# A two-layer RWKV-7 / gated-attention trunk: other accumulators for half units, another order at the attention's entry, and the last scaling split over two engines

## The chip, the cores and the metric

The kernel runs on one core of one Trainium2 chip. The metric is the device time of one execution in microseconds (us). Three runs of the kernel before took 2380.53, 2381.64 and 2383.12 us; their median, 2381.64 us, is what the change is compared with.

## The reference

Sixteen learned tokens stand ahead of 256 real ones, so T = 272 columns go through two layers of width 2048, all in float32:

```
layer 0: h = h + rwkv7(rms_norm(h));  h = h + (relu(rms_norm(h) @ w1) ** 2) @ w2
layer 1: h = h + gla(rms_norm(h));    h = h + (relu(rms_norm(h) @ w1) ** 2) @ w2
out = rms_norm(h)[16:]

gla(x): q, k, v, gate, za = split(x @ w_in)          # za has 16 columns
        glog = log_sigmoid(za @ w_a2 + b_a) / 16      # forget gate of each key dimension
        chunks of 64 tokens: q*exp(cumsum glog), k*exp(-cumsum glog), causal products with v and the state
        out = (per-head norm(o) * silu(gate)) @ w_o
```

The hidden size of the feed-forward part is 8192. Layer 0 ends with the output projection of the RWKV mixer (`w_o`, 2048 x 2048); layer 1 begins with the projection `w_in`, whose last 16 columns (za) feed the forget gate.

## The kernel before

Activations lie transposed: 128 model dimensions on the partitions, tokens along the columns, 16 tiles of 128 dimensions. A product in float32 accuracy is made of three passes over split operands: each 128x1024 piece of weights comes from memory as `raw`, ScalarE rounds it to `hi` (L140), VectorE forms the rest `lo = raw - hi` (L141), and TensorE makes hi*x_hi, hi*x_lo and lo*x_hi (L163, L164, L165; L196 and L197 where two passes are joined). One such piece serves 24 matmuls, some 2.8 us. There are three `raw` buffers, refilled by SP's queue, whose transfers start in the order of that queue when the buffer is free, that is, when VectorE has made the `lo` of its last piece. `hi` and `lo` have two buffers, four inside the gated attention, where two pools take turns.

The order on each engine is fixed when the kernel is built: a scheduler takes the instructions by priority as its own model finds them ready, except inside blocks of manual order (TensorE through the whole RWKV part). `tc.high_priority(offset=...)` pulls the instructions inside it ahead in that choice. On the chip each engine works off its list in order; an instruction that waits holds all that follow it on its engine.

PSUM has eight accumulator banks: `pj` (two), `pm`, `pry` (one each), `pt` and `pu` (two each). A group of products writes one bank, and the next group on this bank waits until VectorE has read it.

**End of the RWKV mixer.** The output projection is cut into units. A half unit `outB(f)` (L907) adds up the last 8 of 16 input tiles for output tile f, on a `pj` bank. A unit `outQ(3, p)` takes 4 input tiles for the two output tiles 2p and 2p+1, on both `pj` banks. The tail of the list is `outB(0), outQ(3,4), outB(1), outB(2), outQ(3,5), outB(3)` and so on to `outB(7)`. Behind each group VectorE adds the bank to the residual (L300), and `done(f)` prepares the next layer's operand for tile f: ScalarE's x_hi (L239) and square (L250), VectorE's x_lo (L240) and the running sum `acc` of squares (L251).

**Entry of the gated attention.** `done` of the first feed-forward part prepares the attention's operand in the same way, and TensorE sums `acc` over the partitions (L255), from which ScalarE makes `rstd`. In `gla` (L1086) the weights `w_a2` of the forget gate are loaded first into a `raw` buffer and split into `wa2`, then za is projected (`pair(48)`), scaled by `rstd` (`zf`), split into `za`, and `gate(0)` and `gate(1)` multiply za by `wa2` on TensorE (L1117) and make the decay factors. Only then come the query and key projections of the first head, `proj(pair(0))` and `proj(pair(8))`.

**The end.** After the last feed-forward part the squares are summed on TensorE (L1316), ScalarE makes `rstd` (L231, L232), and VectorE multiplies the 16 tiles by it in six pieces (L1321); SP sends each piece out when it is made (L1322). GpSimd has no work there.

Of the kernel before, what the change touches and what calls it, by code (L numbers as in the profile page):

```python
# [10 lines left out]
F32 = mybir.dt.float32  # L11
F32R = mybir.dt.float32r
AF = mybir.ActivationFunctionType
ALU = mybir.AluOpType
# [4 lines left out]
P = 128  # L19
D = 2048  # L20
KT = D // P
NMETA = 16
SEQ = 256
T = NMETA + SEQ
# [30 lines left out]
class Kern:  # L55
# [242 lines left out]
    def rwkv(self, done):  # L298
        nc, tc, ap = self.nc, self.tc, self.ap
        tt = lambda o, a, b, op=ALU.mult: nc.vector.tensor_tensor(out=o, in0=a, in1=b, op=op)  # L300
        hres = self.hres
# [58 lines left out]
        pair = lambda w, f: [w[f, 0], w[f, 1]]  # L360
# [5 lines left out]
        with tc.manual_schedule(engines={ENG.PE, ENG.DVE, ENG.Activation}):  # L366
# [51 lines left out]
            for kt in range(KT):  # L418
                w = weight(kt)
                raw, hi, lo = w  # L420
# [484 lines left out]


        def outB(f):  # L907
            ps = self.pj()[:, :T]
            yield from units(yo[8:], 1, ps)
            tt(self.two(hres[:, f]), self.back(ps), self.two(loc[f]), ALU.add)  # L910
            done(f)
            yield
# [173 lines left out]
    def gla(self, x, rstd, hres, done):  # L1086
# [8 lines left out]
        nc.sync.dma_start(gc, ap["gcst"])  # L1095
        mG = gc[:, 0:T]
        mk = [gc[:80, 272:528], gc[:, 528:720], gc[:, 720:784]]
        raw = self.t(self.wp, [P, 1024], "raw", self.raw_bufs)
        nc.sync.dma_start(raw, ap["gla_w_a2"])
        wa2 = self.t(gp, [P, 1024], "wa2", 1, F32R)  # L1100
        nc.scalar.copy(wa2, raw)
        low = slice(64, 96)
        tt(wa2[low], raw[low], wa2[low].bitcast(F32), ALU.subtract)
        zf = self.t(gp, [P, T], "mn", 2)
        tt(self.two(zf), self.proj(pair(48), x, T), self.two(rstd))
        za = self.t(gp, [P, T], "za", 1, F32R)
        nc.scalar.copy(za, zf)
        low = slice(32, 64)
        tt(za[low], zf[low], za[low].bitcast(F32), ALU.subtract)
        rs = rstd[:, NMETA:]  # L1110
        oT = [self.t(self.x2p, [P, 2, T], "x", KT, F32R) for _ in range(KT)]
        c0, c1, c2, c3 = (NMETA + C * i for i in range(4))
# [23 lines left out]
            nc.scalar.activation(dec, dec, AF.Exp, scale=1.0 / TAU)  # L1136
            gates[j] = eb, enb, dec

        for j in range(2):
            gate(j)  # L1140
        for hd in range(GH):
            Q = self.t(gp, [P, 2, 7 * C], "Q", 2)
            KX = self.t(gp, [P, 2, 160 + 6 * C], "KX", 1)
            for dt in range(2):
                j = 2 * hd + dt
                eb, enb, dec = gates.pop(j)
                pq = self.proj(pair(j), x, SEQ, NMETA)
                q, last = Q[:, dt], [eb[:, o + C - 1 : o + C] for o in (c0, c1, c2)]
                qf = self.t(gp, [P, SEQ], "qf", 2)
                nc.vector.scalar_tensor_tensor(out=self.two(qf), in0=pq, scalar=HK ** -0.5, in1=self.two(rs), op0=ALU.mult,  # L1150
                                               op1=ALU.mult)
                tt(q[:, : 3 * C], qf[:, : 3 * C], eb[:, c0:c3])
                tt(q[:, 6 * C :], qf[:, 3 * C :], eb[:, c3:])
                nc.vector.tensor_copy(q[:, 3 * C : 4 * C], q[:, C : 2 * C])
                nc.vector.tensor_scalar(out=q[:, 4 * C : 5 * C], in0=q[:, 2 * C : 3 * C], scalar1=last[1], scalar2=None,
                                        op0=ALU.mult)
                nc.vector.tensor_scalar(out=q[:, 5 * C : 6 * C], in0=q[:, 6 * C :], scalar1=last[2], scalar2=last[1],
                                        op0=ALU.mult, op1=ALU.mult)
                pk = self.proj(pair(8 + j), x, T)
                ks = self.t(gp, [P, T], "ks", 2)  # L1160
                tt(self.two(ks), pk, self.two(rstd))
                kx = KX[:, dt]
                two = lambda x: x.rearrange("p (a t) -> p a t", a=2)
                run = kx[:, 160:]
                tt(kx[:, :NMETA], ks[:, :NMETA], dec[:, :NMETA])
                tt(kx[:, NMETA:80], ks[:, NMETA:c1], enb[:, NMETA:c1])
                tt(two(run[:, : 4 * C])[:, :, :C], two(ks[:, c1:c3]), two(enb[:, c1:c3]))
                tt(run[:, 5 * C :], ks[:, c3:], enb[:, c3:])
                tt(kx[:, 80:160], ks[:, :c1], dec[:, :c1])
                nc.vector.tensor_scalar(out=kx[:, 80 : 80 + NMETA], in0=kx[:, 80 : 80 + NMETA], scalar1=last[0], scalar2=None,  # L1170
                                        op0=ALU.mult)
                tt(run[:, C : 2 * C], ks[:, c1:c2], dec[:, c1:c2])
                nc.vector.tensor_scalar(out=run[:, 3 * C : 4 * C], in0=run[:, C : 2 * C], scalar1=last[2], scalar2=None,
                                        op0=ALU.mult)
                tt(run[:, 4 * C : 5 * C], ks[:, c2:c3], dec[:, c2:c3])
# [97 lines left out]
@with_exitstack  # L1273
def trunk(ctx, tc, ap):
    K = Kern(ctx, tc, ap)
    nc = tc.nc
    out, hres = ap["out"], K.hres
    st = {}

    def operand(gname, off, pool):  # L1280
        def f(kt):
            if kt == 0:
                p = pool()
                st["x"] = [K.t(p, [P, 2, T], "x", KT, F32R) for _ in range(KT)]
                st["acc"] = K.t(K.sp, [P, T], "acc")
            K.prep(K.sp, kt, hres[:, kt, off:], gname, st["x"][kt], st["acc"], T - off)
        return f

    def x2():
        K.x2p = K.sp = ctx.enter_context(tc.tile_pool(name="x2", bufs=1, side="right", reuse_waits="tile"))  # L1290
        return K.x2p

    K.rwkv(operand("norm_mlp0", 0, x2))
    rstd = K.accstd(K.sp, st["acc"], T)
    K.mlp(0, st["x"], rstd, hres, 0, operand("norm_mix1", 0, lambda: K.xp))
    rstd = K.accstd(K.sp, st["acc"], T)
    K.gla(st["x"], rstd, hres, operand("norm_mlp1", NMETA, lambda: K.xp))
    rstd = K.accstd(K.sp, st["acc"], SEQ)

    def last(kt):  # L1300
        if kt == 0:
            st["acc"] = K.t(K.sp, [P, T], "acc")
        h = hres[:, kt, NMETA:]
        if kt < KT - 1:
            K.sqacc(K.sp, kt, h, st["acc"], SEQ)
        else:
            st["sq"] = K.t(K.sp, [P, T], "sq")[:, :SEQ]
            nc.scalar.activation(st["sq"], h, AF.Square)  # L1308
        nc.scalar.mul(h, h, K.vec("norm_f", kt))

    fp = ctx.enter_context(tc.tile_pool(name="fin", bufs=1, side="right"))
    fin = K.t(fp, [P, KT - 2, SEQ], "fin")
    K.mlp(1, st["x"], rstd, hres, NMETA, last)
    ss = K.pm()[:, :SEQ]
    for i, x in enumerate((st["acc"][:, :SEQ], st["sq"])):
        nc.tensor.matmul(ss, K.ones, x, start=i == 0, stop=i == 1)  # L1316
    rstd = K.rstd_from(K.sp, ss, SEQ, 1.0 / D, NORM_EPS, "acc")
    for a, b in ((0, 1), (1, 3), (3, 6), (6, 10), (10, 14), (14, 16)):
        h = hres[:, a:b, NMETA:]
        y = fin[:, a:b] if b < KT else h  # L1320
        nc.vector.tensor_tensor(out=y, in0=h, in1=rstd.unsqueeze(1).to_broadcast([P, b - a, SEQ]), op=ALU.mult)  # L1321
        nc.sync.dma_start(out[:, a:b], y)  # L1322


# [89 lines left out]
```

## Time and profile before

| what | value |
|---|---|
| median of the three runs | 2381.64 us |
| profiled execution, its own time | 2381.23 us |
| its span, first to last instruction | 2379.0 us |
| TensorE busy in the span | 2346.9 us, 99% |
| VectorE busy | 1607.7 us, 68% |
| ScalarE busy | 1260.6 us, 53% |
| GpSimd busy | 12.1 us, 1% |
| granted TensorE clock | 0.999 |

The profiled execution took 2381.23 us, 2.2 us more than its span; what lies outside the span is start and end of the program. "Busy" of TensorE counts matmuls that overlap, so a small step between two matmuls' starts that is longer than usual is time lost, even where the row shows less idle. In the views below a row of the timeline gives the start, the duration, the engine, the line and the tiles (written <- read); brackets at its end give the idle time of the engine before it and who ended it. Rows of waits give: who waited for whom, the total in us, how often, the longest.

### The profile page before, as it was taken

What the parts mean: (1) busy time and instruction counts of PE and PEld (TensorE: products, weight loads), DVE (VectorE), ACT (ScalarE), POOL (GpSimd) and SP (SyncE); (2) the same over time, 40 slices, a digit from 0 to 9 for tenths busy, and PEclk for the clock granted to TensorE, in tenths of its full rate; (3) what the DMA queues carried; (4) which work ended last, traced back from release to release, by engine and by line L of the source; (5) the groups of instructions that cost most, each with busy time, mean ns of one, the idle gap of its engine ahead of it and who ended that gap; (6) DMA issues with size and microseconds to landing.
All of it is one profiled execution on the core that took longest, in us unless ns stands there. A gap on an engine that the chain in (4) does not pass through costs nothing. (4 is left out here: it accounts for less than half of the span.)

```text
span 2379.0 us, 48378 instructions
## 1 busy us (share of the span) xinstructions
PE 2346.9 (99%) x19849; PEld 2224.7 (94%) x19849; DVE 1607.7 (68%) x2702; ACT 1260.6 (53%) x2005; POOL 12.1 (1%) x37
## 2 busy tenths in 40 slices
PE   9999999999999999999999999999999999999998
PEld 8888888889999999999999999999999999999997
DVE  8868986848555555555556777767666666666666
ACT  6478645566555345345345556645555445445444
POOL 0000000000000000000000000000000000000000
PEclk9999999999999999999999999999999999999999
DMA  6469754435555555555555555445555656655554
GB/s 213 154 201 306 245 159 144 143 100 174 186 187 191 190 189 192 187 191 190 188 193 192 188 178 175 162 169 196 183 199 202 204 199 200 203 201 199 203 202 170
DMA packets 157005, 449.20 MB, mean 189 GB/s; under 512 B 33968, under 2 KB 49968, under 8 KB 156784
## 3 DMA queue, kind: packets, MB, share of 16 engines
q1 hardware_dynamic: 156784, 446.11, 56.5%
q8 instruction: 156, 2.56, 0.4%
q14 instruction: 65, 0.53, 0.1%
HBM read 429.93 MB, written 14.42 MB: 187 GB/s over the span
## 5 line engine op out<-in xcount | busy, mean ns | idle before, releaser
L141 DVE TENSOR_TENSOR lo<-raw,hi 128x1024 fp32r<-128x1024 f32 (+1 forms) x818 | 927.7, 1141 | 532.2 <-ACT hi L140 522.1
L140 ACT CAST hi<-raw 128x1024 fp32r<-128x1024 f32 (+1 forms) x818 | 794.1, 978 | 922.4 <-PE pj L164 534.1
L163 PE MATMUL pj<-x,hi 128*128 128x272 f32 (+1 forms) x2624 | 746.5, 284 | 2.6 <-DVE hres L300 1.7
L165 PE MATMUL pj<-x,lo 128*128 128x272 f32 (+1 forms) x2624 | 732.5, 279 | 4.4 <-DVE lo L141 4.3
L164 PE MATMUL pj<-x,hi 128*128 128x272 f32 (+1 forms) x2624 | 731.7, 279 | 0.2 <-DVE x L240 0.2
L163 PEld LDWEIGHTS pj<-x,hi 128*128 128x128 f32 x2624 | 496.9, 189 | 15.8 <-issue 8.2
L165 PEld LDWEIGHTS pj<-x,lo 128*128 128x128 f32 x2624 | 497.0, 189 | 7.0 <-DVE lo L141 6.6
L164 PEld LDWEIGHTS pj<-x,hi 128*128 128x128 f32 x2624 | 497.1, 189 | 2.9 <-issue 1.4
L196 PE MATMUL pj<-x,hi 128*128 128x512 f32 x1280 | 419.8, 382 | 0.1
L197 PE MATMUL pj<-x,lo 128*128 128x256 f32 x1280 | 348.7, 273 | 0.0
L196 PE MATMUL pj<-h,hi 128*128 128x512 f32 x1008 | 330.3, 382 | 0.0
L163 PE MATMUL pj<-h,hi 128*128 128x272 f32 (+1 forms) x1040 | 290.1, 279 | 0.0
L164 PE MATMUL pj<-h,hi 128*128 128x272 f32 (+1 forms) x1040 | 290.1, 279 | 0.0
L165 PE MATMUL pj<-h,lo 128*128 128x272 f32 (+1 forms) x1040 | 290.1, 279 | 0.0
L197 PE MATMUL pj<-h,lo 128*128 128x256 f32 x1008 | 274.8, 273 | 0.0
L196 PEld LDWEIGHTS pj<-x,hi 128*128 128x128 f32 x1280 | 241.9, 189 | 34.1 <-DVE x L1088 0.4
L197 PEld LDWEIGHTS pj<-x,lo 128*128 128x128 f32 x1280 | 245.8, 192 | 0.1
L196 PEld LDWEIGHTS pj<-h,hi 128*128 128x128 f32 x1008 | 190.5, 189 | 26.5
L163 PEld LDWEIGHTS pj<-h,hi 128*128 128x128 f32 x1040 | 196.6, 189 | 0.0
L164 PEld LDWEIGHTS pj<-h,hi 128*128 128x128 f32 x1040 | 196.6, 189 | 0.0
L165 PEld LDWEIGHTS pj<-h,lo 128*128 128x128 f32 x1040 | 196.6, 189 | 0.0
L197 PEld LDWEIGHTS pj<-h,lo 128*128 128x128 f32 x1008 | 193.5, 192 | 0.0
(281 smaller groups left out, 2083.7 us busy)
## 6 DMA issues: line engine op xcount, KB each, us to landing
raw<-mlp_w_d SPq DMA_DIRECT2D x512, 512.0 KB, 3.4
raw<-gla_in_d SPq DMA_DIRECT2D x98, 512.0 KB, 3.3
raw<-w_rkv_d SPq DMA_DIRECT2D x80, 512.0 KB, 3.9
raw<-gla_o_d SPq DMA_DIRECT2D x32, 512.0 KB, 3.3
raw<-w_r_d SPq DMA_DIRECT2D x16, 512.0 KB, 3.3
raw<-rw_oQ_d SPq DMA_DIRECT2D x16, 512.0 KB, 3.4
raw<-lora_d SPq DMA_DIRECT2D x8, 512.0 KB, 3.5
raw<-rw_oA_d SPq DMA_DIRECT2D x8, 512.0 KB, 3.8
```

The costliest lines, as they stand in the source:

```text
L140: nc.scalar.copy(hi[:, h], raw[:, h])
L141: nc.vector.tensor_tensor(out=lo[:, h], in0=raw[:, h], in1=hi[:, h].bitcast(F32), op=ALU.subtract)
L163: nc.tensor.matmul(out, hi[:, ws], xh, start=first, stop=False)
L164: nc.tensor.matmul(out, hi[:, ws], xl, start=False, stop=False)
L165: nc.tensor.matmul(out, lo[:, ws], xh, start=False, stop=last)
L196: nc.tensor.matmul(wide, hi[:, ws], xt, start=kt == 0, stop=False)
L197: nc.tensor.matmul(one, lo[:, ws], xt[:, 0], start=False, stop=kt == nk - 1)
```

## The change

Three edits in one kernel.

1. In `outB(f)` the accumulator is `pry` for odd f and `pm` for even f, in place of a `pj` bank. `outQ` keeps the two `pj` banks.
2. In `gla` the projection of za is called ahead of the load and split of `w_a2`, which get a raised priority; the scaling and split of za get a higher one. The first query projection is called before the gates, `gate(0)` behind it, and `gate(1)` behind the first key projection. The preparation of tile 15 (`done(15)`, at all three borders between parts) gets a raised priority.
3. The last scaling gives its piece of tiles 14 and 15 to GpSimd. VectorE keeps the other five pieces, and SP's queue holds the transfer of GpSimd's piece second instead of last.

```diff
         def outB(f):
-            ps = self.pj()[:, :T]
+            ps = (self.pry if f % 2 else self.pm)()[:, :T]
             yield from units(yo[8:], 1, ps)
...
-        raw = self.t(self.wp, [P, 1024], "raw", self.raw_bufs)
-        nc.sync.dma_start(raw, ap["gla_w_a2"])
-        wa2 = self.t(gp, [P, 1024], "wa2", 1, F32R)
-        nc.scalar.copy(wa2, raw)
-        low = slice(64, 96)
-        tt(wa2[low], raw[low], wa2[low].bitcast(F32), ALU.subtract)
         zf = self.t(gp, [P, T], "mn", 2)
-        tt(self.two(zf), self.proj(pair(48), x, T), self.two(rstd))
+        pz = self.proj(pair(48), x, T)
+        with tc.high_priority(offset=2000):
+            raw = self.t(self.wp, [P, 1024], "raw", self.raw_bufs)
+            nc.sync.dma_start(raw, ap["gla_w_a2"])
+            wa2 = self.t(gp, [P, 1024], "wa2", 1, F32R)
+            nc.scalar.copy(wa2, raw)
+            low = slice(64, 96)
+            tt(wa2[low], raw[low], wa2[low].bitcast(F32), ALU.subtract)
         za = self.t(gp, [P, T], "za", 1, F32R)
-        nc.scalar.copy(za, zf)
         low = slice(32, 64)
-        tt(za[low], zf[low], za[low].bitcast(F32), ALU.subtract)
+        with tc.high_priority(offset=3000):
+            tt(self.two(zf), pz, self.two(rstd))
+            nc.scalar.copy(za, zf)
+            tt(za[low], zf[low], za[low].bitcast(F32), ALU.subtract)
+        pq = self.proj(pair(0), x, SEQ, NMETA)
...
-        for j in range(2):
-            gate(j)
+        gate(0)
...
-                pq = self.proj(pair(j), x, SEQ, NMETA)
+                if j:
+                    pq = self.proj(pair(j), x, SEQ, NMETA)
...
                 pk = self.proj(pair(8 + j), x, T)
+                if j == 0:
+                    gate(1)
...
-            K.prep(K.sp, kt, hres[:, kt, off:], gname, st["x"][kt], st["acc"], T - off)
+            with tc.high_priority(offset=3000) if kt == KT - 1 else ExitStack():
+                K.prep(K.sp, kt, hres[:, kt, off:], gname, st["x"][kt], st["acc"], T - off)
...
-    for a, b in ((0, 1), (1, 3), (3, 6), (6, 10), (10, 14), (14, 16)):
+    for a, b in ((0, 1), (14, 16), (1, 3), (3, 6), (6, 10), (10, 14)):
         h = hres[:, a:b, NMETA:]
         y = fin[:, a:b] if b < KT else h
-        nc.vector.tensor_tensor(out=y, in0=h, in1=rstd.unsqueeze(1).to_broadcast([P, b - a, SEQ]), op=ALU.mult)
+        (nc.gpsimd if b == KT else nc.vector).tensor_tensor(out=y, in0=h, in1=rstd.unsqueeze(1).to_broadcast([P, b - a, SEQ]),
+                                                           op=ALU.mult)
         nc.sync.dma_start(out[:, a:b], y)
```

What the scheduler makes of it is seen in the lists of the engines. On VectorE at the entry of the attention, before (16723 and 16753 are the two halves of za's weights, `wa` is the split of `w_a2`, `hres` and x_15690 belong to tile 15, `acc` is the sum that TensorE's L255 waits for):

```order
L141 TENSOR_TENSOR lo_16724<-raw_16721,hi_16723 128x1024
L213 TENSOR_TENSOR hres_72<-pj_16633,hres_72 128x272
L141 TENSOR_TENSOR lo_16754<-raw_16751,hi_16753 128x1024
L1088 TENSOR_TENSOR wa_2342_16716<-raw_16714,wa_2342_16716 32x1024
L240 SCALAR_TENSOR_TENSOR x_15690<-hres_72,vecs_126,x_15690 128x272
L251 TENSOR_TENSOR acc_15691<-acc_15691,sq_16697 128x272
```

and now (16718 is the first half of za's weights, 16748 the second):

```order
L141 TENSOR_TENSOR lo_16749<-raw_16746,hi_16748 128x1024
L141 TENSOR_TENSOR lo_16719<-raw_16716,hi_16718 128x1024
L213 TENSOR_TENSOR hres_72<-pj_16633,hres_72 128x272
L1088 TENSOR_TENSOR wa_2350_16778<-raw_16776,wa_2350_16778 32x1024
L240 SCALAR_TENSOR_TENSOR x_15690<-hres_72,vecs_126,x_15690 128x272
L251 TENSOR_TENSOR acc_15691<-acc_15691,sq_16697 128x272
```

The same six works stand in another order: both halves of za's weights, the second half first, are ahead of the residual's last add. ScalarE's list has the two casts in the same swapped order, then the cast of `wa`, then tile 15.

On TensorE the first gate product stood inside the first query projection (pj_16841), before:

```order
L163 MATMUL pj_16841<-x_15683,hi_16874 128x256
L164 MATMUL pj_16841<-x_15683,hi_16874 128x256
L1117 MATMUL pm_16801<-za_16782,wa_2342_16716 128x272
L165 MATMUL pj_16841<-x_15683,lo_16875 128x256
L163 MATMUL pj_16841<-x_15684,hi_16874 128x256
```

and stands now behind the whole of it (pj_16785), in front of the key projection (pj_16890):

```order
L164 MATMUL pj_16785<-x_15690,hi_16818 128x256
L165 MATMUL pj_16785<-x_15690,lo_16819 128x256
L1121 MATMUL pm_16862<-za_16781,wa_2350_16778 128x272
L163 MATMUL pj_16890<-x_15675,hi_16893 128x272
L164 MATMUL pj_16890<-x_15675,hi_16893 128x272
```

It moved behind 22 matmuls of the second half of that projection; the second gate product moved from the same projection to the end of the key projection.

On SP's queue at the end of the program, before:

```order
L1322 DMA out_d<-fin_21670 128x256
L1322 DMA out_d<-fin_21670 128x512
L1322 DMA out_d<-fin_21670 128x768
L1322 DMA out_d<-fin_21670 128x1024 x2
L1322 DMA out_d<-hres_72 128x2x256
```

and now:

```order
L1330 DMA out_d<-fin_21670 128x256
L1330 DMA out_d<-hres_72 128x2x256
L1330 DMA out_d<-fin_21670 128x512
L1330 DMA out_d<-fin_21670 128x768
L1330 DMA out_d<-fin_21670 128x1024 x2
```

The transfer of tiles 14 and 15 (`hres`), now GpSimd's piece, moved from the last place to the second.

## The prediction

> **What bounds the kernel now.** I read the page first, then TensorE's waits, then the timeline of TensorE and of those it waits for at each place that the change touches.
>
> ```profile
> span 2379.0 us, 48378 instructions
> PE 2346.9 (99%) x19849; PEld 2224.7 (94%) x19849; DVE 1607.7 (68%) x2702; ACT 1260.6 (53%) x2005; POOL 12.1 (1%) x37
> ```
>
> TensorE is busy 99% of the span, and the change removes none of its matmuls. It can win only what TensorE stands idle, plus what comes after the last matmul. TensorE's longest waits at the places of the change are these:
>
> ```profile
> PE pm L1117 <- DVE za L1088: 1.3, 1, 1.3
> PE pj L163 <- DVE hres L300: 1.7, 4, 0.7
> PE pm L255 <- DVE acc L251: 1.0, 1, 1.0
> PE pj L164 <- DVE x L240: 0.2, 1, 0.2
> ```
>
> They sum to 4.2 us, under 0.2% of the time: the whole change is about a few us, and the signs of small waits matter.
>
> **Part 1: own banks for the half units.** The timeline of TensorE and VectorE at the end of the third of the four unit pairs:
>
> ```profile
> 589.01 0.28 PE L165 MATMUL pj<-x,lo 128*128 128x272 f32 x1
> 589.64 0.35 PE L163 MATMUL pj<-x,hi 128*128 128x272 f32 x1 [0.35 <-DVE hres L300]
> 589.05 0.78 DVE L300 TENSOR_TENSOR hres<-pj,r 128x272 f32<-128x272 f32 x2
> ```
>
> Matmuls of this shape start 0.116 us apart elsewhere (589.01 against the one in front of it). Here it is 0.63: TensorE, through with an `outQ`, wants its first bank for the next `outB`, and VectorE reads that bank only from 589.05. This costs 0.51, and the first matmul behind it takes 0.08 more. The same stands at 571.16 and 580.08, and a small form of it (0.24) at 562.58: 3 x 0.59 + 0.24 = 2.0 us. With `pm` and `pry` nothing has to be read first: their last users are VectorE's and ScalarE's reads of the unit before the last, some 5 us earlier. So these waits go. What is late next is VectorE itself:
>
> ```profile
> 560.00:596.00 36.00, 34.75 (x291) 33.87 (x290) 33.63 (x69) 25.74 (x55) 0.00 (x0) 1.00 0.53 177
> ```
>
> (columns: stretch, length, busy time of PE, PEld, DVE, ACT, POOL.) VectorE is busy 33.6 of 36 us. From one double add to the next (580.13 to 589.05) it takes 8.9 us, with some 0.3 idle, so it needs 8.6; TensorE needs 72 x 0.116 = 8.35. VectorE falls behind by 0.25 us in each of three rounds. A `lo` is ready some 1.3 us before TensorE needs it, which covers that lag until the last tile: the next part's first group needs tile 7, whose add is VectorE's last.
>
> ```profile
> 592.69 0.44 DVE L300 TENSOR_TENSOR hres<-pj,hres 128x272 f32<-128x272 f32 x1
> 593.71 1.23 DVE L141 TENSOR_TENSOR lo<-raw,hi 128x1024 fp32r<-128x1024 f32 x1 [0.23 <-ACT hi L140]
> 594.85 0.50 DVE L240 SCALAR_TENSOR_TENSOR x<-hres,vecs,x 128x272 fp32r<-128x272 f32 x1
> 595.40 0.38 PE L164 MATMUL pj<-x,hi 128*128 128x272 f32 x1 [0.20 <-DVE x L240]
> ```
>
> `outB(7)` ends about 2.0 us earlier, near 590.4. I followed VectorE's and ScalarE's new lists with these spacings: the add at about 591.3, `lo` (its cast waits for TensorE's release of the buffer, as now) from 591.8, one sum, then x_lo from about 593.3 to 593.8. TensorE goes on at 593.8, against 595.40. **Gain 1.6.** Bounds: 2.0 if VectorE's lag costs nothing, 1.0 if VectorE sets the pace all through (3 x 0.3 and a little). The raised priority of tile 15 at this border swaps two of VectorE's short works; at the border behind the attention all lists are as before: nothing.
>
> **Part 2: the attention's entry.** TensorE's rows there, in order of time:
>
> ```profile
> 1305.33 0.28 PE L165 MATMUL pj<-x,lo 128*128 128x272 f32 x1
> 1308.46 0.28 PE L165 MATMUL pj<-x,lo 128*128 128x272 f32 x1
> 1309.77 0.72 PE L255 MATMUL pm<-acc,cst 128*128 128x272 f32 x2 [1.03 <-DVE acc L251]
> 1312.53 0.28 PE L164 MATMUL pj<-x,hi 128*128 128x256 f32 x1
> 1312.79 0.38 PE L165 MATMUL pj<-x,lo 128*128 128x256 f32 x1
> 1315.46 0.28 PE L164 MATMUL pj<-x,hi 128*128 128x256 f32 x1
> 1317.00 0.40 PE L1117 MATMUL pm<-za,wa 128*128 128x272 f32 x1 [1.26 <-DVE za L1088]
> ```
>
> Starts that lie 1.31, 0.26 and 1.54 apart where 0.11 is usual: 1.19 + 0.25 (0.15, and 0.1 in the matmul behind) + 1.43 = 2.87 us lost between the first matmul of za's projection and the end of the first query projection. What the new order does to each:
>
> ```profile
> 1302.49 1.05 ACT L140 CAST hi<-raw 128x1024 fp32r<-128x1024 f32 x1 [1.07 <-PE pj L165]
> 1305.28 1.05 ACT L140 CAST hi<-raw 128x1024 fp32r<-128x1024 f32 x1 [1.74 <-DMA raw<-gla_in_d]
> 1306.23 1.04 ACT L1101 CAST wa<-raw 128x1024 fp32r<-128x1024 f32 x1
> 1303.57 1.23 DVE L141 TENSOR_TENSOR lo<-raw,hi 128x1024 fp32r<-128x1024 f32 x1 [0.88 <-ACT hi L140]
> 1309.28 0.43 DVE L251 TENSOR_TENSOR acc<-acc,sq 128x272 f32<-128x272 f32 x1
> 1304.82 0.33 SPq L132 DMA_DIRECT2D raw<-gla_in_d  x1
> ```
>
> *The sum of squares.* Tile 15's add ends at 1305.74, yet `acc` is made at 1309.28, because the cast and split of `wa` and the second half's weights stand ahead. With the weights loaded one transfer earlier, the cast of `wa` ends near 1306.3, its split near 1307.6, and `acc` is ready near 1308.4. L255 now stands 5 matmuls earlier in TensorE's list, near 1308.7: no wait. *The gate.* L1121 stands behind the whole query projection, near 1317.6; za is ready near 1316 by the same spacings: no wait, 1.43 gone.
>
> *A new wait: the first weights.* ScalarE now casts the second half first, from 1302.49 (when its transfer lands), and VectorE splits it first. The half that TensorE needs at 1305.33 comes second: cast 1303.44 to 1304.49, split 1304.72 to 1305.95, so TensorE waits until about 1306.0. Cost 0.6; bounds 0.2 (transfer 0.4 earlier) and 0.8. *Another: the query's weights.* Their transfer started at 1304.82, when a buffer was free; now it starts when that late split ends, at 1305.95. How long it takes is the open point:
>
> ```profile
> raw<-gla_in_d SPq DMA_DIRECT2D x98, 512.0 KB, 3.3
> 1310.43 1.05 ACT L140 CAST hi<-raw 128x1024 fp32r<-128x1024 f32 x1 [2.42 <-DMA raw<-gla_in_d]
> ```
>
> The median is 3.3 us, but this very transfer took until 1310.43, 5.6 us, with the constants' 392 KB right behind it. If it lands at L, TensorE can use the `lo` at L + 2.4 (cast 1.05, split 1.23, hand-over), and wants it at 1312.05: a wait of L - 1309.63, from 0 (3.3 us) to 1.9 (5.6). I take the middle, 0.6 (L = 1310.2). **Gain 2.87 - 0.6 - 0.6 = 1.65**, bounds 2.65 and 0.2.
>
> **Part 3: the end.** VectorE's scaling, SP's last issue and the landing times:
>
> ```profile
> 2370.06 4.17 DVE L1321 TENSOR_TENSOR fin<-hres,acc 128x256 f32<-128x256 f32 x5 [2.19 <-ACT acc L232]
> 2374.15 0.69 DVE L1321 TENSOR_TENSOR hres<-hres,acc 128x512 f32<-128x512 f32 x1
> 2374.90 0.38 SPq L1322 DMA_DIRECT2D out_d<-hres  x1
> out_d<-fin SPq DMA_DIRECT2D x2, 512.0 KB, 2.8
> out_d<-hres SPq DMA_DIRECT2D x1, 256.0 KB, 3.0
> ```
>
> VectorE without its last piece ends at 2374.23, and the last transfer, now one of 512 KB, would land at 2374.25 + 2.8 = 2377.05, against 2374.90 + 2.98 = 2377.88: 0.8 gained, if the engines don't disturb each other. They do in this trace, where a GpSimd copy meets a VectorE product of two SBUF operands:
>
> ```profile
> 115.97 0.19 POOL L651 COPY WC<-W 128x4 f32<-128x4 f32 x1 [101.38 <-ACT W L633]
> 177.34 0.36 POOL L651 COPY WC<-W 128x4 f32<-128x4 f32 x1 [6.26 <-ACT W L633]
> 177.22 0.51 DVE L300 TENSOR_TENSOR bk<-kk,iW 128x256 f32<-128x256 f32 x2
> L322 POOL MEMSET ar<- 128x576 f32 x1 | 0.6, 577 | 0.0
> ```
>
> Alone the copy takes 0.19; beside the product it takes 0.36 and ends at 177.70, just behind the first of the two products (0.42 long, to 177.64). So it waited for the product's end and then went ahead of the rest. All pieces of the last scaling are such products. I take it that the lock holds both ways: GpSimd starts behind VectorE's first piece (2370.49), and VectorE's second waits for GpSimd's end. GpSimd's product of 512 columns appears in no row: a memset writes 576 columns in 0.58, so 512 take 0.5 at the least, and with two operands read one after the other 1.05, which I take; 1.5 is the upper bound. VectorE's other four pieces (3.83 from 2370.40) then run 2371.54 to 2375.37, the last transfer starts at 2375.43 and lands at 2378.2. **Loss 0.4**; bounds -0.8 (no lock) and +0.9 (1.5 us).
>
> The Trainium skill, page "SBUF — State Buffer", section "Who interferes with whom", states the lock: a VectorE instruction with two SBUF inputs and a GpSimd one that reads SBUF exclude each other for the whole instruction. The copy's 0.36 agrees; that VectorE waits in turn no row here shows. From "GPSIMD Engine Reference", section "Performance versus the Vector engine" (4497 ns for 2048 columns), I estimate 1.1 us for this product, and the loss would be 0.45.
>
> **The sum.** -1.6 - 1.65 + 0.4 = -2.85. Against the profiled execution's 2381.23 (span 2379.0 and 2.2 around it) that is 2378.4. The median of the runs is 0.4 above that execution, so I predict 2381.64 - 2.85 = **2378.8 us**.
>
> **Rivals.**
> - *No lock at the end.* The 0.8 comes as gain: -4.05, **2377.6**. For it: the copy is the only such meeting, 4 columns long, and VectorE was not seen held. Against: it did wait.
> - *The weights eat the entry's gain.* L near 1311.5 and the late first half: entry -0.3, total -1.5, **2380.1**. For it: 5.6 us for this transfer before. Against: it then had an earlier start beside the same constants.
> - *All goes well:* -2.0 - 2.65 - 0.8 = -5.4, **2376.2**. It needs three bounds at once.
> - *SP's queue behind GpSimd, slower than before.* SP's second transfer waits for GpSimd alone, and four of six transfers, with it 1.9 of 2.1 MB, stand at or behind that wait. If GpSimd gets its turn only when VectorE is through (2374.23) and needs 1.05, it ends at 2375.3; at the 0.4 MB per us that the last transfers reach, all land about 5.75 later, at 2381.0, 3.2 later than now, which cancels the rest. Any further delay counts in full: with 1.5 us more, **2383**. It decides from an end of GpSimd's product at 2375.4 on. For it: GpSimd has done no product before this one, and VectorE's pieces follow without a gap. Against: the copy got its turn behind one product. The Trainium skill ("GPSIMD Engine Reference", section "Instruction dispatch") gives about 6 us for the first call of freshly loaded code; no row here shows one.
>
> **How the numbers follow.** Chances: forecast 0.50, no lock 0.16, weights 0.14, all well 0.10, SP behind GpSimd 0.10. What a measurement can tell from no change is 0.2%, 4.8 us: below 2376.9 lies most of "all well" and the edge of "no lock" (0.14), above 2386.4 a third of the last rival (0.04), the rest is no change (0.82). The range 2376.6 to 2381.3 leaves out the lower half of "all well" and nearly all of the slow rival. My median's own uncertainty, some 1 us by the three runs, lies in it.
>
> **What would show it.** Right: no wait of L163 on L300 near 571, 580 and 589; x_lo of tile 7 as the next wait; no wait at L255 and L1121; a new wait of L165 on `lo` near 1305 (about 0.6) and another at the query's first `lo`; GpSimd's product of about 1.1 us behind VectorE's first piece, and a hole of that length between VectorE's first and second. Wrong: waits on `lo` between 562 and 590, the query's weights landing later than 1311, a GpSimd product that ends behind VectorE's last piece or one beside which VectorE runs on.

## The result

| | before | changed |
|---|---|---|
| median, 21 runs each | 2382.23 us | 2378.79 us |
| profiled execution | 2381.23 us | 2377.58 us |
| its span | 2379.0 us | 2375.3 us |

The ratio is 0.9986, with a 95% interval of 0.998 to 0.9992: the kernel became faster by 3.4 us, between 1.9 and 4.8. The prediction said 2.85, and took 4.8 us for the least that could be told from no change; with 21 runs of each kernel the interval leaves zero out at 3.4. Since all terms are small, the stretches tell more than the total. In TensorE's records the same matmul is found in every kernel by its number. Between fixed ones these times pass, worked out from the starts in the two profiled executions (the first row starts at the first matmul, 1.4 us into the span):

| stretch | before | changed | difference |
|---|---|---|---|
| start to the half units (code unchanged) | 552.60 | 551.89 | -0.71 |
| half units (380 matmuls) | 46.71 | 45.07 | -1.64 |
| first feed-forward part | 704.38 | 704.38 | 0 |
| entry of the attention (399 matmuls from za's first) | 48.95 | 46.97 | -1.98 |
| the rest, to VectorE's first last scaling | 1016.01 | 1016.42 | +0.41 |
| the end | 8.92 | 9.18 | +0.26 |

The changed places give -1.64 - 1.98 + 0.26 = -3.36, close to the difference of the medians. The -0.71 and the +0.41 lie where the instructions are the same; section "What was not expected" returns to them.

The page of the changed kernel, and TensorE's waits in it:

```profile
span 2375.3 us, 48373 instructions
PE 2344.9 (99%) x19849; PEld 2224.1 (94%) x19849; DVE 1607.3 (68%) x2701; ACT 1259.7 (53%) x2005; POOL 13.6 (1%) x38
```

```profile
PE pj L165 <- DVE lo L141: 5.0, 8, 1.8
PE pj L163 <- DVE hres L300: 0.7, 1, 0.7
PE pj L164 <- DVE x L240: 0.5, 1, 0.5
```

L163's waits for `hres` fell from four (1.7 us) to one, and that one lies outside the half units. The waits at L255 and at the gate product have left the list. In exchange L165 waits once more for a `lo`, 0.7 us, and x_lo (L240) costs 0.5 in place of 0.2.

**The half units.** The timeline of TensorE and VectorE at the same place as before (the clock of this execution runs 0.7 us ahead here):

```profile
586.90 0.28 PE L165 MATMUL pj<-x,lo 128*128 128x272 f32 x1
587.02 0.28 PE L163 MATMUL pry<-x,hi 128*128 128x272 f32 x1
590.50 0.43 DVE L300 TENSOR_TENSOR hres<-pry,hres 128x272 f32<-128x272 f32 x1
590.96 1.22 DVE L141 TENSOR_TENSOR lo<-raw,hi 128x1024 fp32r<-128x1024 f32 x1
592.46 0.50 DVE L240 SCALAR_TENSOR_TENSOR x<-hres,vecs,x 128x272 fp32r<-128x272 f32 x1
593.01 0.38 PE L164 MATMUL pj<-x,hi 128*128 128x272 f32 x1 [0.50 <-DVE x L240]
```

The first matmul of the half unit starts 0.12 behind the one in front of it, no longer 0.63. The stretch ends with the wait for tile 7's x_lo: the add at 590.50, the `lo`, one sum, x_lo, and TensorE goes on at 593.01. That is 593.7 on the clock of before, where it was 595.40.

**The entry.** Rows of TensorE, ScalarE, VectorE and SP (this execution is 2.34 us ahead of before at za's first matmul):

```profile
1300.39 1.99 ACT L140 CAST hi<-raw 128x1024 fp32r<-128x1024 f32 x2 [1.31 <-DMA raw<-gla_in_d]
1301.47 2.36 DVE L141 TENSOR_TENSOR lo<-raw,hi 128x1024 fp32r<-128x1024 f32 x2 [1.11 <-ACT hi L140]
1302.72 1.47 SPq L132 DMA_DIRECT2D raw<-gla_in_d  x2
1302.88 0.28 PE L164 MATMUL pj<-x,hi 128*128 128x272 f32 x1
1303.88 0.38 PE L165 MATMUL pj<-x,lo 128*128 128x272 f32 x1 [0.73 <-DVE lo L141]
1304.10 0.28 PE L163 MATMUL pj<-x,hi 128*128 128x272 f32 x1
1305.90 1.05 ACT L140 CAST hi<-raw 128x1024 fp32r<-128x1024 f32 x1 [0.83 <-DMA raw<-gla_in_d]
1306.03 0.43 DVE L251 TENSOR_TENSOR acc<-acc,sq 128x272 f32<-128x272 f32 x1
1306.65 0.62 PE L255 MATMUL pm<-acc,cst 128*128 128x272 f32 x2
1315.13 0.30 PE L1121 MATMUL pm<-za,wa 128*128 128x272 f32 x1
```

Neither L255 nor L1121 has a bracket: both waits are gone. The two halves of za's weights are cast and split as one run, the second half first, and TensorE's L165 starts 1.00 behind the matmul in front where 0.116 is usual, the next one 0.22: the new wait costs 1.0. The query's weights are cast at 1305.90 with no wait of TensorE behind them.

**The end.** The groups of the scaling line, and the chain of waits through it (start, us, what):

```profile
L1328 DVE TENSOR_TENSOR fin<-hres,acc x5: 426/1211/1751, 2366.2 to 2370.2; 128x1024 f32<-128x1024 f32 x2, 128x256 f32<-128x256 f32 x1, 128x512 f32<-128x512 f32 x1, 128x768 f32<-128x768 f32 x1
L1328 POOL TENSOR_TENSOR hres<-hres,acc x1: 1498/1498/1498, 2366.2 to 2366.2; 128x512 f32<-128x512 f32 x1
```

```profile
2366.15 0.43 DVE fin L1328
2366.58 1.67 DVEq L1417
2368.24 3.14 DVE fin L1328 x3
```

GpSimd's product is recorded from 2366.20 to 2367.70, but VectorE's first piece runs to 2366.58, so 1.12 us of it are work. VectorE's longest piece is now one of 1751 ns: it is the second, of 512 columns. Before, the group's longest was 1221 ns, a piece of 1024 columns, and 512 columns took 0.69:

```profile
L1321 DVE TENSOR_TENSOR fin<-hres,acc x5: 426/951/1221, 2370.1 to 2373.0; 128x1024 f32<-128x1024 f32 x2, 128x256 f32<-128x256 f32 x1, 128x512 f32<-128x512 f32 x1, 128x768 f32<-128x768 f32 x1
```

The second piece is 1.06 longer, about as long as GpSimd's work. SP's last issue came 4.83 after the first piece's start before and comes 5.26 after it now.

```profile
2371.41 0.33 SPq L1330 DMA_DIRECT2D out_d<-fin  x1
```

GpSimd's sequencer (POOLq) has two more instructions for this line; they stand in every kernel that gives it the product and in no other, 1867 us ahead of the product:

```profile
L1328 POOLq MODIFY_POOL_CONFIG  x2: 4/4/4, 498.9 to 498.9; - x2
```

### The profile page after: what moved, and what is told of

Read it like the earlier page. It is cut to its first block, busy times and chain, and to the rows that moved or that the text cites. A ratio compares the mean times of both kernels' runs of the same rounds, so it can differ in the third digit from the quotient of the medians.

```text
span 2375.3 us, 48373 instructions
## 1 busy us (share of the span) xinstructions
PE 2344.9 (99%) x19849; PEld 2224.1 (94%) x19849; DVE 1607.3 (68%) x2701; ACT 1259.7 (53%) x2005; POOL 13.6 (1%) x38
## 5 line engine op out<-in xcount | busy, mean ns | idle before, releaser
L163 PE MATMUL pj<-x,hi 128*128 128x272 f32 (+1 forms) x2560 | 728.1, 284 | 1.6 <-DVE r L300 0.9
L165 PE MATMUL pj<-x,lo 128*128 128x272 f32 (+1 forms) x2560 | 714.8, 279 | 5.1 <-DVE lo L141 5.0
L164 PE MATMUL pj<-x,hi 128*128 128x272 f32 (+1 forms) x2560 | 713.8, 279 | 0.5 <-DVE x L240 0.5
L163 PEld LDWEIGHTS pj<-x,hi 128*128 128x128 f32 x2560 | 484.8, 189 | 14.1 <-issue 6.5
L165 PEld LDWEIGHTS pj<-x,lo 128*128 128x128 f32 x2560 | 484.9, 189 | 7.8 <-DVE lo L141 7.5
L164 PEld LDWEIGHTS pj<-x,hi 128*128 128x128 f32 x2560 | 485.0, 189 | 3.2 <-issue 1.4
L163 PE MATMUL pj<-h,hi 128*128 128x272 f32 (+1 forms) x1040 | 290.1, 279 | 0.0
L165 PE MATMUL pj<-h,lo 128*128 128x272 f32 (+1 forms) x1040 | 290.1, 279 | 0.0
L196 PEld LDWEIGHTS pj<-x,hi 128*128 128x128 f32 x1280 | 241.9, 189 | 33.9 <-DVE x L1088 0.4
L197 PEld LDWEIGHTS pj<-x,lo 128*128 128x128 f32 x1280 | 245.8, 192 | 0.1
L163 PEld LDWEIGHTS pj<-h,hi 128*128 128x128 f32 x1040 | 196.6, 189 | 0.0
L165 PEld LDWEIGHTS pj<-h,lo 128*128 128x128 f32 x1040 | 196.6, 189 | 0.0
```

What stands on the lines that cost most here:

```text
L163: nc.tensor.matmul(out, hi[:, ws], xh, start=first, stop=False)
L164: nc.tensor.matmul(out, hi[:, ws], xl, start=False, stop=False)
L165: nc.tensor.matmul(out, lo[:, ws], xh, start=False, stop=last)
L196: nc.tensor.matmul(wide, hi[:, ws], xt, start=kt == 0, stop=False)
L197: nc.tensor.matmul(one, lo[:, ws], xt[:, 0], start=False, stop=kt == nk - 1)
```

## The experiments

Each was timed in 5 rounds (11 runs) beside the kernel before, on the same chip. "Half units", "entry" and "end" are the three stretches of the table above, from each kernel's profile.

| kernel | median less before | ratio, 95% interval | half units | entry | end |
|---|---|---|---|---|---|
| before | | | 46.71 | 48.95 | 8.92 |
| changed | -3.4 | 0.998 to 0.9992 | 45.07 | 46.97 | 9.18 |
| e1, banks alone | -2.6 | 0.9983 to 1.0 | 45.07 | 48.33 | 8.91 |
| e2, entry alone | -1.5 | 0.9985 to 1.0002 | 47.05 | 48.65 | 8.93 |
| e3, end alone | -0.4 | 0.9991 to 1.0009 | 46.71 | 49.80 | 9.17 |
| e4, without the third edit | -4.7 | 0.9973 to 0.999 | 45.07 | 47.11 | 8.91 |
| e5, halves in turn | -5.0 | 0.9973 to 0.9991 | 45.07 | 46.30 | 8.93 |
| e6, factor in a bank | -3.5 | 0.9979 to 0.9997 | 45.07 | 46.71 | 9.53 |
| e7, list order at the end | -4.3 | 0.9976 to 0.9994 | 45.07 | 46.95 | 9.16 |
| e8, no raised tile 15 | -3.7 | 0.9978 to 0.9995 | 45.07 | 46.68 | 9.17 |
| e9, own queue | -4.0 | 0.9976 to 0.9994 | 45.07 | 47.49 | 9.14 |
| e10, e5 with e9's end | -5.1 | 0.997 to 0.9988 | 45.07 | 47.07 | 8.71 |

The intervals are some 4 us wide in all: the medians separate the kernels with both of the first two edits from the one before, and not the kernels from each other; e1 and e2, with one of the two, reach 1.0. The verdicts below rest on the stretches.

### The banks alone

```diff
-            ps = self.pj()[:, :T]
+            ps = (self.pry if f % 2 else self.pm)()[:, :T]
```

> The kernel before with the first edit alone: outB on pm and pry, everything else as before. If the banks alone give the first term (theory), TensorE's L163 no longer waits for VectorE's L300 near 571, 580 and 589, x_lo of tile 7 is the next wait (0.5 us or less), and between the matmuls at 562 and 593 TensorE gains 1.6 us (bounds 1.0 to 2.0); the median falls by 1.6. Rival: the gain needs the raised priority of tile 15, which swaps two works of VectorE at this border; then less than 1.2 us is gained here and a wait on x_lo of 1 us or more stands at the end of the stretch.

TensorE's waits between 540 and 600 us, before and here:

```profile
PE pj L163 <- DVE hres L300: 1.0, 3, 0.3
PE pj L164 <- DVE x L240: 0.2, 1, 0.2
```

```profile
PE pj L164 <- DVE x L240: 0.5, 1, 0.5
```

The stretch takes 45.07, to the hundredth what it takes in every kernel with this edit. The theory holds: the banks alone give 1.64.

### Tile 15 not raised

```diff
-            with tc.high_priority(offset=3000) if kt == KT - 1 else ExitStack():
+            with ExitStack():
```

> The changed kernel without the raised priority of tile 15's preparation. The lists differ at one place alone: VectorE and ScalarE swap two short works of tiles 14 and 15 near 589 us. Theory: within 0.2 us of the changed kernel between the matmuls at 580 and 600. Rival: x_lo of tile 15 comes 0.4 us later and TensorE waits for it that much longer.

45.07 again: with the new banks the raised priority is worth nothing here. Without them it costs: in e2, where it meets the old banks, the stretch took 47.05, which is 0.34 more than before.

### The entry alone

The kernel before with the second edit.

> The kernel before with the second edit alone: the entry of the attention in the new order and the raised priority of tile 15; banks and end as before. If the entry stands by itself (theory), TensorE gains 1.9 to 2.2 us between the first matmul of za's projection and the end of the second key projection: the waits at L255 (1.19), at a query lo (0.25) and at the gate product (1.43) are gone, and a new wait of 0.9 to 1.0 for the first half's lo stands at the second-half-first swap. The median falls by 2.0. Rival: the stretch gains by luck of one execution's transfers, and the query's weights land late here; then a second wait of L165 of 0.6 us or more stands at the query's projection and the gain is 1.4 or less.

Its gain is as small as the rival's, though not by the wait that the rival named: no second wait of L165 stands at the query's projection. TensorE's waits between 1300 and 1330 us:

```profile
PE pj L165 <- DVE lo L141: 0.9, 1, 0.9
PE pm L1121 <- DVE mn L1128: 0.7, 1, 0.7
PE pj L163 <- ACT hi L140: 0.3, 1, 0.3
```

The first half's wait is there as expected, but TensorE also waited 0.44 for that half's `hi`, just ahead of the stretch, and the second gate product waited for VectorE. The entry took 48.65, which with the 0.44 is no gain at all over the profile of before. So one execution doesn't give this term. All profiles together do better: three with the old entry (before, e1, e3) took 48.95, 48.33 and 49.80, a mean of 49.0; the seven with the new one (changed, e2, e4, e6, e7, e8, e9) took 46.68 to 48.65, a mean of 47.2. The gain is 1.8 on that (2.0 without e2, the only one of the seven above 47.5; 1.7 without e2 and e3, the slowest on either side). Why e2's weights came late is open: its lists at this place are those of e4, and I didn't test it further.

### The end alone, and without it

e3 is the kernel before with the third edit; e4 is the changed kernel with the six pieces on VectorE again, in the old order.

> The kernel before with the third edit alone. Theory (VectorE is held while GpSimd multiplies): GpSimd's product shows some 1.5 us, of which 0.4 is waiting behind VectorE's first piece, VectorE's second piece shows 1.7 in place of 0.69, and from the first piece to the end of the span 9.15 us pass in place of 8.94: 0.2 to 0.4 us slower than the kernel before. Rival (the work is shared): 8.1 us, 0.8 faster.

> The changed kernel with the third edit undone: VectorE scales all six pieces in the old order. If VectorE is held for the whole of GpSimd's product (theory), this kernel is 0.2 to 0.4 us faster than the changed one: from the first piece of the scaling to the end of the span 8.94 us as before, against 9.15 with GpSimd. Rival (no lock, VectorE's second piece was slow for another reason): the sharing gains 0.8, and this kernel is 0.8 us slower than the changed one. The median is 3.5 to 4 us below the kernel before by the theory, some 2.8 below by the rival.

The end took 9.17 with GpSimd and 8.91 without it. Both agree with the changed kernel and with the one before to 0.01, so the third edit costs 0.26, whatever stands ahead of it. The rival's 0.8 is out. e4's median is 1.3 below the changed kernel's, of which the profiles explain the 0.26; the rest is within what these medians leave open.

### What VectorE's second piece waits for

```diff
-    rstd = K.rstd_from(K.sp, ss, SEQ, 1.0 / D, NORM_EPS, "acc")
+    lnr = K.t(K.sp, [P, SEQ], "acc")
+    nc.scalar.activation(lnr, ss, AF.Ln, scale=1.0 / D, bias=K.eps[NORM_EPS])
+    rps = K.pry()[:, :SEQ]
+    nc.scalar.activation(rps, lnr, AF.Exp, scale=-0.5)
+    nc.scalar.activation(lnr, lnr, AF.Exp, scale=-0.5)
...
-        (nc.gpsimd if b == KT else nc.vector).tensor_tensor(out=y, in0=h, in1=rstd.unsqueeze(1).to_broadcast([P, b - a, SEQ]),
+        (nc.gpsimd if b == KT else nc.vector).tensor_tensor(out=y, in0=h, in1=(lnr if b == KT else rps).unsqueeze(1).to_broadcast([P, b - a, SEQ]),
```

> The changed kernel with the factor rstd made twice: ScalarE writes it first to an accumulator bank, from which VectorE reads it, then to SBUF, from which GpSimd reads it (0.43 us of ScalarE more ahead of GpSimd). VectorE's pieces so have one SBUF operand. Theory (the two exclude each other only while VectorE reads two SBUF operands): VectorE's second piece shows 0.7 to 0.8 and not 1.7, GpSimd's product runs beside it in some 1.1 us, and the last issue comes 0.9 to 1.1 us earlier after the first piece than in the changed kernel; the end gains 0.5 to 1.0 us over it. Rival (they exclude each other whatever VectorE reads, or the second piece waits for something else, such as the memory that both write): the second piece again shows 1.7 and the end gains nothing, or loses some 0.1 for the slower bank.

The groups of the scaling line and the issues of the last transfers:

```profile
L1332 DVE TENSOR_TENSOR fin<-hres,pry x5: 420/946/1212, 2369.5 to 2372.5; 128x1024 f32<-128x1024 f32 x2, 128x256 f32<-128x256 f32 x1, 128x512 f32<-128x512 f32 x1, 128x768 f32<-128x768 f32 x1
L1332 POOL TENSOR_TENSOR hres<-hres,acc x1: 1267/1267/1267, 2370.0 to 2370.0; 128x512 f32<-128x512 f32 x1
```

```profile
2371.33 0.40 SPq L1334 DMA_DIRECT2D out_d<-hres  x1
2371.78 2.40 SPq L1334 DMA_DIRECT2D out_d<-fin  x4
```

The first half of the theory is shown: VectorE's longest piece is one of 1024 columns again (1212), the second takes 0.68, and GpSimd works beside it in 1.27. With the factor in a bank nothing holds VectorE, so it was held by what it read in SBUF beside the residual. That this is the second operand in SBUF, and not the one tile of the factor that both engines read in the changed kernel and no longer share here, e6 alone doesn't separate; the copy that was held at 177.34 in the kernel before shared no tile with VectorE's product. The second half fell: VectorE is through 1.09 us earlier (4.15 after its first start, and 5.23 in the changed kernel), and yet the end takes 9.53, longer than with the lock. VectorE's next piece is ready at 1.02, but SP stands at GpSimd's transfer until 1.79, and issues the four others behind it (2371.78 is 2.24 after the first start). This is the mechanism of the prediction's slow rival, in a small form. Of the 0.35 by which e6 ends later than the changed kernel, the landings make 0.17 (SP goes on behind them 8.31 after the first piece's start, and 8.14 in the changed kernel); the rest stands behind the landings, where ScalarE's last step ends at 9.31 in place of 8.75, and no transfer explains it.

### A queue of its own for GpSimd's piece

```diff
-        nc.sync.dma_start(out[:, a:b], y)
+        (nc.scalar if b == KT else nc.sync).dma_start(out[:, a:b], y)
```

> The kernel e6 (factor from an accumulator bank for VectorE) with the transfer of GpSimd's piece on ScalarE's queue, so that SP's four later transfers no longer stand behind GpSimd's product. In e6 VectorE was through 4.15 us after the start of its first piece (5.23 in the changed kernel), yet the span ended 9.53 after it (9.18). Theory: SP's second issue, held until 1.79, made a hole in the transfers, and 1.97 MB at some 0.4 MB per us then set the end; with the queue free, SP issues near 0.51, 1.06, 1.92, 3.05 and 4.17 and the span ends 8.2 to 8.8 after the first piece's start, ahead of the kernel before's 8.92. Rival: the transfers' rate alone sets the end, whenever they start; then the span still ends 9.2 or later after it.

SP now issues at 0.50, 1.05, 1.91, 3.04 and 4.17, as the theory wanted, and the end takes 9.14: more than the theory's 8.8, a little less than the rival's 9.2. The moved GB/s in 40 slices of the last 15 us and the issues by group here, and the issues of the changed kernel's last 13 us:

```profile
GB/s 0 0 0 0 0 0 0 0 0 0 0 0 0 254 210 371 230 410 366 377 322 407 407 415 393 415 415 404 197 22 0 0 0 0 0 0 0 22 0 0
...
out_d<-fin SPq DMA_DIRECT2D x2, 512.0 KB, 3.9
out_d<-fin SPq DMA_DIRECT2D x1, 384.0 KB, 2.6
...
out_d<-hres ACTq DMA_DIRECT2D x1, 256.0 KB, 3.5
```

```profile
out_d<-fin SPq DMA_DIRECT2D x2, 512.0 KB, 2.8
out_d<-fin SPq DMA_DIRECT2D x1, 384.0 KB, 2.5
out_d<-hres SPq DMA_DIRECT2D x1, 256.0 KB, 2.2
```

The last two transfers were issued a microsecond sooner and took a microsecond longer. The 16 DMA engines move some 0.4 MB per us here, and 2.1 MB need 5.3 us at that rate; making the pieces sooner doesn't shorten that. But the rate isn't the whole. In e10 the same end, issued at the same times to 0.02 us, took 8.71, inside the theory's range. The row of GB/s over the same stretch of e10:

```profile
GB/s 0 0 0 0 0 0 0 0 0 0 0 0 0 254 200 382 221 325 407 396 374 391 448 371 404 437 382 404 197 0 0 0 0 0 0 22 0 0 0 0
```

Both rows fall off with 404 and 197, and in e9 a slice with 22 GB/s follows, in which e10 moves none of its output: the last three packets of 4 KB end 7.34 to 7.65 us after the first piece's start in e9, and all others by 7.26; in e10 all end by 7.27, in the kernel before by 7.41. That is 0.39 of the 0.43 between the two ends. A load of 8 KB of instructions took 0.31 us among e9's transfers (2371.34 to 2371.65) and none fell among e10's; that it made the delay isn't shown. So the ends without the lock took 9.53, 9.14 and 8.71, around the 8.92 of before: with a queue of its own GpSimd's piece may win 0.2 us, less than these medians could tell.

One attempt at this queue gave nothing: e7 put GpSimd's piece last in the program's order, but SP's list, which the scheduler orders by its own model, still had its transfer second.

> The changed kernel with GpSimd's piece issued last in SP's queue and made in the old place of the list, still by GpSimd. GpSimd's product depends on nothing but rstd, so it still starts behind VectorE's first piece and holds the second: VectorE's four pieces end as in the changed kernel (5.23 us after the first one's start). Theory: only the order of the transfers differs, 256 KB last in place of 512 KB, and the end moves by 0.3 us or less. Rival (SP's queue behind GpSimd costs something): this kernel is 0.5 us or more faster than the changed one.

It is the changed kernel once more, with the same issues and an end of 9.16. Whether the place in SP's queue alone costs something was not tried.

### The halves in turn

```diff
-        self.wps.append(es.enter_context(tc.tile_pool(name="wp2", bufs=1)))
+        wp2 = es.enter_context(tc.tile_pool(name="wp2", bufs=1))
...
-        pz = self.proj(pair(48), x, T)
+        pz = self.proj(pair(48), x, T); self.wps.append(wp2)
```

> The kernel e4 (third edit undone) with both halves of za's weights in the first of the two pools of hi and lo buffers; the second pool joins behind them. ScalarE then casts the first half first, as TensorE needs it, and the split of w_a2 falls behind tile 15's sum of squares; the constants' transfer goes one place ahead of the query's second half. If the swapped order alone makes the new wait (theory), the wait of L165 for the first half's lo (1.01 between two starts, 0.22 behind it) is gone and the kernel gains 1.0 us more than e4, some 4.8 below the kernel before. Rival: TensorE then only comes 1.0 earlier to the query's second half, whose lo was ready some 0.2 us ahead of need in the changed kernel and now has the constants' 392 KB ahead of its transfer; a wait of 0.8 us or more on that lo takes the gain back, and the kernel is within 0.3 us of e4.

The lists had the second half first because its `hi` lies in the second pool, which is free at this point, while the first half's `hi` waits for TensorE to release a buffer of the first pool. With both in the first pool they come in turn. The rows at za's first matmuls, and TensorE's waits between 1300 and 1325 us:

```profile
1301.00 1.23 DVE L141 TENSOR_TENSOR lo<-raw,hi 128x1024 fp32r<-128x1024 f32 x1 [0.84 <-ACT hi L140]
1305.29 0.43 DVE L251 TENSOR_TENSOR acc<-acc,sq 128x272 f32<-128x272 f32 x1
1305.78 0.73 PE L255 MATMUL pm<-acc,cst 128*128 128x272 f32 x2 [0.26 <-DVE acc L251]
```

```profile
PE pm L255 <- DVE acc L251: 0.3, 1, 0.3
```

The first `lo` is ready at 1302.2 and TensorE doesn't wait for it; no wait for the query's second half takes its place, so the rival falls. But L255 stands early enough to wait 0.54 less 0.12 for `acc`: of the 1.0, some 0.6 should be left, and the stretch is 0.7 shorter (46.30 against 46.99, the mean of the six other profiles with the swapped halves, e2 left out). Part of that is a later wait that e5 happens not to have (next section). To the matmul ahead of that wait, e5 and e10, the two with the halves in turn, took 38.19 and 38.20, and the six took 38.58 to 38.96, a mean of 38.69: 0.5 is what the order of the halves gives.

### Both together

e10 is e5 with the end of e9.

> The kernel e5 (banks, new entry with the halves in turn) with the end of e9 (factor from a bank, GpSimd's transfer on ScalarE's queue). Theory: the terms add; TensorE's part is that of e5, 5.2 us ahead of the kernel before in its profile at the last matmul (of which some 0.9 was gained ahead of the change's places), the end gives 0.2 to 0.7 on top, and the median is 5.0 to 5.8 us below the kernel before. Rival: the end gives nothing and the median is that of e5, 4.5 to 5.0 below.

Its median lies 5.1 below the kernel before, e5's 5.0: no difference that these medians could tell. In its profile the end is 0.22 shorter than e5's, as the theory's lower bound wanted, but its entry is 0.77 longer. A wait made that (between 1318 and 1350 us):

```profile
PE pt L1231 <- DVE Am L1088: 0.6, 1, 0.6
```

This is further on in the first head. VectorE's masked product is late because it stands behind the split of a piece of weights, whose cast waited for its transfer:

```profile
1338.35 1.04 ACT L140 CAST hi<-raw 128x1024 fp32r<-128x1024 f32 x1 [2.37 <-DMA raw<-gla_in_d]
1339.43 1.23 DVE L141 TENSOR_TENSOR lo<-raw,hi 128x1024 fp32r<-128x1024 f32 x1 [1.41 <-ACT hi L140]
```

Counted from the 220th of the stretch's 399 matmuls, inside the second key projection, this cast starts after 8.54 us in the three profiles with the old entry, and after 9.38 to 10.34 in the nine with the new one. Up to 9.58 (e5, e6, e8) TensorE doesn't wait; from 9.78 on (the six others) it does, and longer the later the cast. From that matmul to the end of the stretch the three profiles with the old entry took 20.56; with the new one it was 20.56 in e5, e6 and e8, 20.75 in the changed kernel, and up to 21.32 in e10. So the new entry uses up a slack of about a microsecond here, and how late this piece of weights comes decides whether TensorE loses nothing or up to 0.8 us. What makes it come so differently stays open. The version to keep is e5: the first two edits with the halves in turn, and VectorE's old end. That it is ahead of e4 rests on the stretches; the medians differ by 0.2.

## Why the prediction was right

The time came out where it was forecast, 2378.8, and the gain 0.6 us larger than forecast, with the interval of 1.9 to 4.8 around both. That the time was met to the hundredth is luck: the three runs from whose median the gain was taken off lay 0.6 below the 21 of the result (2381.64 against 2382.23), which made up for the gain's 0.6. Inside the entry, too, errors of up to 0.6 went both ways. By its steps:

- **The banks: right, in mechanism and size.** Forecast 1.6, measured 1.64 in each of the nine profiles with the new banks. VectorE takes over as the limit, and the wait for tile 7's x_lo ends the stretch: TensorE was to go on at 593.8, and went on at 593.7 on the same clock.
- **Tile 15's priority at this border: nothing, as forecast.** That it depends on the banks (0.34 lost without them) was not seen.
- **L255 and the gate product: right.** Both waits are gone. L255 came without any wait here. In other profiles with the new entry that isn't always so: L255 waited 0.4 in e9, and the second gate product 0.7 in e2.
- **The first half's weights: right mechanism, too small.** Forecast 0.6 with an upper bound of 0.8, measured 1.0 here and 0.75 to 1.22 in the seven profiles with the swapped halves. The second half's transfer landed 0.24 later than assumed (cast from 1302.73 on the clock of before, against 1302.49), which moved both casts and splits, and the matmul behind the wait took another 0.1.
- **The query's weights: the step that failed.** The prediction had their transfer start "when that late split ends, at 1305.95". It started at 1305.06 on the clock of before (the row of 1302.72), 0.03 after the split that ended first: the buffer handed on was the one of the half split first, not that of the first half. In all twelve profiles this transfer starts 0.03 behind the end of the split that ended first, whichever half it was. It landed in 3.2 us, and there was no wait, nor was there one at the query's `lo` in any profile with the new entry. That term of 0.6 was void.
- **What was missing at the entry:** the wait at L1231 behind it, 0.2 in this profile with what follows it, and up to 0.8 in others (e10). On the other side the old waits cost more than was counted. Behind each of the two gate products the next matmul started 0.23 later where 0.116 is usual, and the second matmul of L255 started 0.33 behind the first, against 0.23 now: 0.3 in all. With the query's 0.6 gone, the first half's extra 0.4, the 0.2 at L1231 and this 0.3, the forecast of 1.65 (its terms give 1.67) becomes the 1.98 of this profile; the mean over profiles is 1.8.
- **The lock at the end: right in both directions.** GpSimd waited for VectorE's first piece, worked 1.12 us (1.05 was taken) and held the second piece for 1.06. The Trainium skill's statement on this ("SBUF — State Buffer", section "Who interferes with whom") agrees with the trace, now for VectorE's side too (0.69 against 1.75), and so does its condition of two SBUF operands (0.68 with one of them in a bank). The estimate of 1.1 us from the Trainium skill ("GPSIMD Engine Reference", section "Performance versus the Vector engine") is that of the trace. The first call of some 6 us, which the prediction named from the same page of the Trainium skill (section "Instruction dispatch"), did not show, but this product doesn't test it: a load of code behind the two early instructions of its line (at 498.9) would be long over when it starts.
- **The loss at the end: 0.26 against 0.4.** SP's last issue came 5.26 after the first piece's start, and 5.37 was worked out.
- **The rivals.** "No lock" priced the free end at a gain of 0.8, and that price was wrong even without a lock: the ends of e6, e9 and e10 lie 0.61 above, 0.22 above and 0.21 below the 8.92 of before. The 2.8 us of landing were taken from transfers that had 256 KB less ahead of them; the two of 512 KB took 3.9 in e9 and 3.4 in e10. "All goes well" falls with it. "SP's queue behind GpSimd" did not decide in the changed kernel, where GpSimd got its turn early, and cost a few tenths in e6, not 3 us.

## What to carry to other kernels

A wait that is removed on one engine is worth what the next late engine leaves: follow the new list to the next bracket, and the gain comes out to a tenth, as with the banks. Before an idle engine is given a share of a last step, ask whether its operands exclude the other engine and whether the transfers behind it are the bound already: here the first was so, and the second left 0.2 us to win at best. And where two buffers of a pair lie in pools of which one is free sooner, a scheduler may take the second half first; here, giving both the same pool put them in turn and won 0.5 us.

## What was not expected

Up to the half units all kernels run the same instructions, yet the profiles took 551.4 to 555.5 us to that point. What makes these 4 us was not looked into. Behind the entry the identical part took 1016.0 in six profiles of twelve, 0.4 more in five and 0.9 more in one. In the chain of waits one late piece of feed-forward weights stands behind each 0.4, two behind the 0.9 (e10), and none in the six; in the changed kernel it is this one:

```profile
2192.32 6.11 DMA raw<-mlp_w_d
2200.89 0.38 PE pj L197
```

The median transfer of these takes 3.4 us, and this one 6.11; in e1, e3, e6, e8 and e10 the chain shows others of 6.1 to 6.3, in e1, e8 and e10 the same piece near the end, in the others at other places. Why single transfers come late, no run here shows. Both parts together are a scatter of a few us in which a change of this size has to be found, and that is why stretches between fixed matmuls were compared.
